# One pool of 2 KB slices for activations and split weights, and c loaded as one row, in a two-layer decoder trunk

## The chip, the cores and the metric

The kernel runs on one core of one Trainium2 chip. The metric is the time of one execution on the device in microseconds (us); lower is better. The engines are TensorE (PE in the profile; its weight loads are PEld), VectorE (DVE), ScalarE (ACT), GpSimd (POOL) and SyncE (SP), which issues nearly all transfers. SBUF, the working memory, is 128 partitions wide. PSUM, the matmul's output, has eight banks of 128 x 512 f32.

## The reference

Two layers act on x, 512 x 1024 f32. Each layer is a SwiGLU FFN with half weight, a token mixer, and a second such FFN. The mixer of layer 0 is a latent attention with 16 heads, and that of layer 1 is a dilated window attention with three groups of 16 heads. Each of the six sub-layers is wrapped in the same way:

```
mod = silu(c) @ w_mod[i] + b_mod[i]          # c: 1 x 1024, shift, scale, gate for each sub-layer
hn  = rmsnorm(x, pre_g) * (1 + scale) + shift
y   = rmsnorm(fn(hn), post_g)
x   = x + res_w * gate * y                   # res_w: 0.5 for FFNs, 1 for mixers

swiglu(h) = (silu(h @ w_gate) * (h @ w_up)) @ w_down      # D_FF = 2816
```

All inputs and parameters are f32.

## The kernel before

**Split products.** Every large product is three matmuls in a reduced f32 format (`mm3`, L141 to L146): both operands are split into a high part (a rounded copy) and a low part (the value minus the high part), and high x high, high x low and low x high are added in PSUM. The weights are split on the chip. `weights` (L123) loads a 128 x 1024 f32 block (512 KB) into a `raw` buffer (five of them), makes the high part with one ACT copy of 1024 columns (L128), and the low part with two DVE subtractions of 512 columns (L130). The parts go to the pool `ring`, six places of 4 KB per partition for `whi` and six for `wlo`. A second form, `Sliced` (L53 to L75), writes the parts as 512-column slices of 2 KB into the pool `sl` instead; it is used for the first weights of a sub-layer.

**The slices.** `sl` has 44 places of 2 KB (`t.s()`, L111). The modulated input h takes 16 (eight row blocks, high and low), the sub-layer's output y 8, a group of gated FFN rows up to 12, and the attention layers keep their queries, keys and values there.

**FFN.** The 22 column blocks of the hidden layer are taken in four groups (`GROUPS`). For each block, `head` forms gate and up products over eight k (48 matmuls of 512 columns) and the gated result. After a group, `down` adds its product with `w_down` for four row tiles. The last group's `down` is the tail of the sub-layer; `transition` (L458) weaves it with the norm of x, the turn of the next input (`turn`, L490: transposes on PE, then `modulate`), and the first heads of the next sub-layer.

**Order.** A planner (the Tile framework) orders each engine's instructions by the program's order and by its own estimate of when each can run, and places tiles in the pools. In `start` (L332) the order of SP, and for a stretch that of ACT and DVE, is as written out by hand.

**The start.** SP fetches c, broadcast to 128 partitions (512 KB written, L379), x tiles 0 and 1, the small vectors, the first block of `w_mod` for shift, x tile 2, the first block for scale, x tile 3, and both halves of the two weights of unit 0 (gate and up of block 0). ACT takes the silu of c (L396). `rise` (L352) handles one 128-row tile of x: ACT sums its squares, DVE adds them (L313), POOL raises to the power -1/2 (L314), DVE scales the tile (L364, L368), PE transposes it into eight PSUM banks (L370). `mod_fold` (L162) forms the dot of a `w_mod` block with the silu of c on DVE (L165) and adds the bias at once (`mod_out`, L168, L210). It stands behind tile 1 for shift and behind tile 2 for scale. Then the first 128 rows (k = 0) are modulated (L301 to L303), unit 0's halves are split (L68, L72), and `keep` (L374) copies the other banks to slices. Behind that a loop brings, for each further k, the four half blocks of `w_mod` (`mod_load`, L170), their dots (L180), the modulation, and the products of all units loaded so far; units 1 to 3 join after k = 1, 2 and 3.

```
rise(0); rise(1)
self.mod_fold(*mods[0], 0, raw[0])
rise(2)
self.mod_fold(*mods[1], 0, raw[1])
rise(3)
```

Of the kernel before, what the change touches and what calls it, by code (L numbers as in the profile page):

```python
# [24 lines left out]
RAW = 5  # L25
SLICES = 44
SLOTS = 6
KQ = 2
# [14 lines left out]

class Halves:
    def __init__(self, parts):
        self.parts = [x.rearrange("p (k c) -> p k c", c=P) for x in parts]

# [4 lines left out]

class Sliced:  # L53


    def __init__(self, t, src):
        self.t, self.src = t, src
        self.raw = t.ring.tile([P, CH], F32, tag="raw", name="raw", bufs=RAW)
        self.out = [[t.s(F32R), t.s(F32R)] for _ in range(2)]

    def at(self, j):
        return slice(j * SEQ, (j + 1) * SEQ)

    def fetch(self, j):
        self.t.nc.sync.dma_start(self.raw[:, self.at(j)], self.src[:, self.at(j)])

    def top(self, j):
        self.t.nc.scalar.activation(self.out[0][j], self.raw[:, self.at(j)], AF.Copy)  # L68

    def low(self, j):  # L70
        hi, lo = self.out
        self.t.nc.vector.tensor_tensor(lo[j], self.raw[:, self.at(j)], f(hi[j]), ALU.subtract)  # L72

# [4 lines left out]
class Trunk:  # L78
    def __init__(self, ctx, tc, a):
        self.ctx, self.tc, self.nc, self.a = ctx, tc, tc.nc, a  # L80
        nc = tc.nc
        self.cp = ctx.enter_context(tc.tile_pool(name="const", bufs=1))
        self.ring = ctx.enter_context(tc.tile_pool(name="ring", bufs=SLOTS))
        self.sl = ctx.enter_context(tc.tile_pool(name="sl", bufs=SLICES))
# [37 lines left out]

    def weights(self, src, flat=False):  # L123
        raw = self.load(src)
        n = src.shape[-1]
        hi = self.ring.tile([P, CH], F32R, tag="whi", name="whi")[:, :n]
        lo = self.ring.tile([P, CH], F32R, tag="wlo", name="wlo")[:, :n]
        self.nc.scalar.activation(hi, raw, AF.Copy)  # L128
        for r in (slice(0, n // 2), slice(n // 2, n)):
            self.nc.vector.tensor_tensor(lo[:, r], raw[:, r], f(hi[:, r]), ALU.subtract)  # L130
# [28 lines left out]
    def mod(self, l, n, k):  # L159
        self.mod_fold(l, n, k, self.load(self.a["w_mod"][l, n, k]))  # L160

    def mod_fold(self, l, n, k, raw):  # L162
        nc = self.nc
        t = self.tmp.tile([P, 2], F32, tag="mt", name="mt", bufs=4)
        nc.vector.tensor_tensor_reduce(  # L165
            raw, raw, self.cs, 1.0, 0.0, ALU.mult, ALU.add, accum_out=t[:, 0:1]
        )
        self.mod_out(l, n, k, t, lambda out, b: nc.vector.tensor_tensor(out, t[:, 0:1], b, ALU.add))  # L168

# [162 lines left out]
    def start(self, sub):  # L332
# [19 lines left out]
        def rise(i):  # L352
# [8 lines left out]
            else:  # L361
                self.square(x[1], t[1], ss[:, 1:2])
            r = self.scale_of(ss)
            nc.vector.tensor_scalar(t[0], x[0], r, None, ALU.mult)  # L364
            if last:
# [12 lines left out]
        self.first = sub  # L378
        nc.sync.dma_start(self.cs, self.a["c"].broadcast_to([P, D]))  # L379
# [12 lines left out]
        xt = [self.bank("mm" if k < 4 else "aux") for k in range(KT)]  # L392
        units, ks = [], []
        banks = {}
        with self.tc.manual_schedule(engines={ACT, DVE}):
            nc.scalar.activation(self.cs, self.cs, AF.Silu)  # L396
# [109 lines left out]
class Ffn:  # L506
# [10 lines left out]

    def gate_up_load(self, ft, sliced=False):
        t = self.t
        make = t.weights_sliced if sliced else t.weights  # L520
        self.w[ft] = [make(t.a["w_gu"][self.l, self.s, ft, g]) for g in range(2)]

    def prepare(self):
        self.gate_up_load(0, True)

# [49 lines left out]
    def down(self, q, i):  # L575
# [3 lines left out]
        if q not in self.wd:  # L579
            self.wd[q] = [  # L580
                t.weights(t.a["w_down"][self.l, self.s, at + j], flat=True) for j in range(m)
            ]
# [48 lines left out]
class Mixer:  # L631
# [5 lines left out]
    def out_weights(self, j):  # L637
        t = self.t
        if j not in self.wo:
            self.wo[j] = t.weights(t.a[self.w_o][j], flat=True)  # L640

    def products(self, b, i, d, js):
        t = self.t
        for j in js:
# [3 lines left out]
                [x[j][:, i * P : (i + 1) * P] for x in self.o],  # L648
                [x[:, d * SEQ : (d + 1) * SEQ] for x in self.wo[j]],
                j in (0, PART),  # L650
# [34 lines left out]
class Mla(Mixer):  # L685
# [37 lines left out]
    def prepare(self):  # L723
        self.w = {u: self.t.weights_sliced(self.t.a["mla_in"][u]) for u in range(2)}

# [30 lines left out]
    def value(self, j, e):  # L756
        t = self.t
        if not self.wv:
            self.wv += [t.weights(t.a["mla_v"][k], flat=True) for k in range(2)]
        b = t.bank()  # L760
        for k in range(2):
            ls = [x[:, j * P : (j + 1) * P] for x in self.latn[k]]
            t.mm3(b, ls, [x[:, e * SEQ : (e + 1) * SEQ] for x in self.wv[k]], k == 0, k == 1)
        self.v[j, e] = t.s()
# [163 lines left out]
class Dil(Mixer):  # L928
# [78 lines left out]
    def prepare(self):  # L1007
        t = self.t
        self.wt = {(0, u): t.weights_sliced(t.a["dil_in"][0, u]) for u in self.ORDER[:2]}

# [390 lines left out]
```

## Time and profile before

| | |
|---|---|
| time, median of 3 runs | 2277.34 us (2276.07 to 2277.81) |
| the profiled execution's own time | 2277.64 us |
| its span | 2275.9 us |
| PE busy | 2241.0 us, 98% |
| PE weight loads busy | 1853.5 us, 81% |
| DVE busy | 1203.6 us, 53% |
| ACT busy | 861.4 us, 38% |
| POOL busy | 106.1 us, 5% |
| mean granted clock of TensorE | 0.998 of full |

The span is the stretch that the profiler recorded; the time is a little longer. A row of the timeline has the start and the length in us, the engine, the source line, the operation, output and inputs, the shape and the count; in brackets stands how long the engine was idle before it and what ended that idle time. A row of the waits has engine, tile and line, what it waited for, and then the total in us, the number of times and the longest. A row of the groups has the busy time and the mean ns of one, and behind the bar the idle time before them and what ended it. A row of the stretches has the length, then the busy time (and count) of PE, PEld, DVE, ACT and POOL, the granted clock, the share of the transfer engines and GB/s. A row of the transfers has the count, the size, and the median us from issue to landing.

### The profile page before, as it was taken

The page shows a single profiled execution, that of the slowest core. Times are in us where ns is not written, and L with a number is a line of the kernel's source. Part 1 is how long each engine was busy: PE and PEld are TensorE (multiplying, and loading weights), DVE is VectorE, ACT ScalarE, POOL GpSimd, SP SyncE. Part 2 cuts the span into 40 slices and gives each one's busy share as a digit, 9 for nine tenths or more (in the row PEclk, how much of TensorE's full clock was granted, in tenths as well). Part 3 has the DMA queues.
Part 4 walks back from the last instruction along what each step waited for, and adds up shares of the span by engine and source line. Part 5 has one row for each costly group of instructions (what it writes and reads, how often), then busy time and mean ns, then how long its engine had stood idle before and what let it go on. Part 6 is the DMA issues. An engine that isn't in the chain of part 4 may idle for free. (4 is left out here: it accounts for less than half of the span.)

```text
span 2275.9 us, 30179 instructions
## 1 busy us (share of the span) xinstructions
PE 2241.0 (98%) x11418; PEld 1853.5 (81%) x11418; DVE 1203.6 (53%) x2711; ACT 861.4 (38%) x1751; POOL 106.1 (5%) x143
## 2 busy tenths in 40 slices
PE   6999999999999999999999999999999999999998
PEld 5888888877898888898888888777878878888887
DVE  7666566677665366474554473344334367243344
ACT  4432135577633132353222352444344345332232
POOL 0000001210110000020000010000000002000000
PEclk9999999999999999999999999999999999999999
DMA  8575662211255365344653523333333332242231
GB/s 311 162 251 183 186 231 69 99 47 56 70 172 184 93 208 176 107 140 123 192 175 114 155 93 105 80 95 88 83 89 80 96 79 79 75 130 98 79 111 37
DMA packets 121366, 284.56 MB, mean 125 GB/s; under 512 B 44145, under 2 KB 48516, under 8 KB 121220
## 3 DMA queue, kind: packets, MB, share of 16 engines
q1 hardware_dynamic: 121220, 282.63, 40.5%
q8 instruction: 89, 1.46, 0.3%
q14 instruction: 57, 0.47, 0.1%
HBM read 280.19 MB, written 2.39 MB: 124 GB/s over the span
## 5 line engine op out<-in xcount | busy, mean ns | idle before, releaser
L143 PE MATMUL mm<-s,whi 128*128 128x512 f32 (+1 forms) x2116 | 797.8, 378 | 3.7 <-ACT whi L128 2.5
L144 PE MATMUL mm<-s,whi 128*128 128x512 f32 (+1 forms) x2116 | 792.2, 374 | 0.0
L145 PE MATMUL mm<-s,wlo 128*128 128x512 f32 (+1 forms) x2116 | 791.5, 374 | 0.0
L128 ACT ACTIVATE whi<-raw 128x1024 fp32r<-128x1024 f32 (+1 forms) x356 | 369.7, 1053 | 973.2 <-PE mm L144 441.8
L130 DVE TENSOR_TENSOR wlo<-raw,whi 128x512 fp32r<-128x512 f32 (+1 forms) x712 | 466.0, 693 | 409.9 <-ACT whi L128 401.7
L143 PEld LDWEIGHTS mm<-s,whi 128*128 128x128 f32 x2116 | 399.3, 189 | 84.4 <-issue 7.0
L145 PEld LDWEIGHTS mm<-s,wlo 128*128 128x128 f32 x2116 | 399.6, 189 | 70.9
L144 PEld LDWEIGHTS mm<-s,whi 128*128 128x128 f32 x2116 | 399.5, 189 | 67.8
L143 PE MATMUL mm<-whi,s 128*128 128x512 f32 x848 | 332.4, 392 | 2.0 <-ACT s L679 1.3
L144 PE MATMUL mm<-wlo,s 128*128 128x512 f32 x848 | 330.4, 390 | 0.0
L145 PE MATMUL mm<-whi,s 128*128 128x512 f32 x848 | 330.1, 389 | 0.0
L165 DVE CUSTOM_DVE_ANT_0 raw<-raw,cs 128x1024 f32<-128x1024 f32 x130 | 160.1, 1236 | 108.5 <-DMA raw<-w_mod 107.9
L143 PEld LDWEIGHTS mm<-whi,s 128*128 128x128 f32 x848 | 159.2, 188 | 36.6 <-issue 2.5
L145 PEld LDWEIGHTS mm<-whi,s 128*128 128x128 f32 x848 | 159.2, 188 | 33.4 <-issue 0.3
L144 PEld LDWEIGHTS mm<-wlo,s 128*128 128x128 f32 x848 | 159.2, 188 | 32.6 <-issue 0.3
L554 DVE TENSOR_TENSOR gg<-silu,mm 128x512 f32<-128x512 f32 (+1 forms) x95 | 60.4, 635 | 172.2 <-PE mm L145 168.8
L444 DVE TENSOR_TENSOR s<-mm,s 128x512 f32<-128x512 f32 x112 | 76.5, 689 | 124.8 <-PE mm L145 124.7
L314 POOL TENSOR_TENSOR mv<-mv,mhalf 128x1 f32<-128x1 f32 x48 | 35.9, 750 | 1498.9 <-DVE mv L313 1496.4
L555 ACT ACTIVATE s<-gg 128x512 fp32r<-128x512 f32 (+1 forms) x97 | 57.4, 591 | 53.3 <-DVE gg L554 53.2
L552 ACT ACTIVATE silu<-mm 128x512 f32<-128x512 f32 (+1 forms) x95 | 51.4, 543 | 30.6 <-PE mm L145 30.5
L1040 ACT ACTIVATE s<-mm 128x512 f32<-128x512 f32 (+3 forms) x156 | 46.2, 374 | 34.8 <-PE mm L145 34.8
L448 ACT ACTIVATE s<-mm 128x512 f32<-128x512 f32 x40 | 23.8, 595 | 85.8 <-PE mm L145 85.5
(165 smaller groups left out, 1738.1 us busy)
## 6 DMA issues: line engine op xcount, KB each, us to landing
raw<-w_gu SPq DMA_DIRECT2D x168, 512.0 KB, 4.4
raw<-w_mod SPq DMA_DIRECT2D x130, 512.0 KB, 4.7
raw<-w_down SPq DMA_DIRECT2D x88, 512.0 KB, 4.3
raw<-dil_in SPq DMA_DIRECT2D x70, 512.0 KB, 3.6
s<-w_mod SPq DMA_DIRECT2D x28, 256.0 KB, 6.6
raw<-w_gu SPq DMA_DIRECT2D x16, 256.0 KB, 3.2
raw<-mla_o SPq DMA_DIRECT2D x8, 512.0 KB, 4.7
raw<-dil_o SPq DMA_DIRECT2D x8, 512.0 KB, 3.7
```

Source lines behind the costliest of these rows:

```text
L128: self.nc.scalar.activation(hi, raw, AF.Copy)
L130: self.nc.vector.tensor_tensor(lo[:, r], raw[:, r], f(hi[:, r]), ALU.subtract)
L143: mm(out, w[0], m[0], start=first, stop=False)
L144: mm(out, w[0], m[1], start=False, stop=False)
L145: mm(out, w[1], m[0], start=False, stop=last)
L165: nc.vector.tensor_tensor_reduce(raw, raw, self.cs, 1.0, 0.0, ALU.mult, ALU.add, accum_out=t[:, 0:1])
L314: nc.gpsimd.tensor_tensor(v[:, 1:2], v[:, 0:1], self.mhalf[:, 0:1], ALU.pow)
L444: nc.vector.tensor_tensor(y, b, y, ALU.add)
L552: nc.scalar.activation(s, banks[0], AF.Silu)
L554: nc.vector.tensor_tensor(v, s, banks[1], ALU.mult)
L555: nc.scalar.activation(ghi, v, AF.Copy)
L1040: nc.scalar.activation(out, src, AF.Copy)
```

## The change

The two forms of splitting become one. `Sliced` is renamed `Weights` and serves all weights: one fetch of the whole block, then for each half of 512 columns one ACT copy and one DVE subtraction into 2 KB slices. The pool `sl` has 68 places in place of 44; `whi` and `wlo` have no places any more. Products that read a weight by halves (`down`, the mixers' output products, `value`) take the slice of that half.

In the start, c is fetched as one row of 4 KB; two PE matmuls with a row of ones copy it to all partitions in two PSUM banks, and the silu reads it there in two halves. The fetches are in another order: row, x tile 0, shift block, x tile 1, scale block, x tiles 2 and 3, the small vectors, and the first halves of unit 0. The dot for shift stands behind tile 0 and that for scale behind tile 1. The bias sums of both stand in the last tile's `rise`, behind the request for its power. The second halves of unit 0 are fetched and split ahead of unit 2's weights.

```diff
-SLICES = 44
-SLOTS = 6
+SLICES = 68
-class Sliced:
+class Weights:
...
-    def fetch(self, j):
-        self.t.nc.sync.dma_start(self.raw[:, self.at(j)], self.src[:, self.at(j)])
+    def fetch(self, *js):
+        c = slice(self.at(js[0]).start, self.at(js[-1]).stop)
+        self.t.nc.sync.dma_start(self.raw[:, c], self.src[:, c])
...
-    def weights(self, src, flat=False):
-        raw = self.load(src)
-        n = src.shape[-1]
-        hi = self.ring.tile([P, CH], F32R, tag="whi", name="whi")[:, :n]
-        lo = self.ring.tile([P, CH], F32R, tag="wlo", name="wlo")[:, :n]
-        self.nc.scalar.activation(hi, raw, AF.Copy)
-        for r in (slice(0, n // 2), slice(n // 2, n)):
-            self.nc.vector.tensor_tensor(lo[:, r], raw[:, r], f(hi[:, r]), ALU.subtract)
-        return [t if flat else t.rearrange("p (k c) -> p k c", c=P) for t in (hi, lo)]
-
-    def weights_sliced(self, src):
-        w = Sliced(self, src)
+    def weights(self, src):
+        w = Weights(self, src)
+        w.fetch(0, 1)
         for j in range(2):
-            w.fetch(j)
             w.top(j)
             w.low(j)
         return w.parts()
...
+    def mod_dot(self, raw):
         nc = self.nc
         t = self.tmp.tile([P, 2], F32, tag="mt", name="mt", bufs=4)
         nc.vector.tensor_tensor_reduce(
             raw, raw, self.cs, 1.0, 0.0, ALU.mult, ALU.add, accum_out=t[:, 0:1]
         )
-        self.mod_out(l, n, k, t, lambda out, b: nc.vector.tensor_tensor(out, t[:, 0:1], b, ALU.add))
+        return t
+
+    def mod_sum(self, l, n, k, t):
+        add = self.nc.vector.tensor_tensor
+        self.mod_out(l, n, k, t, lambda out, b: add(out, t[:, 0:1], b, ALU.add))
...
             r = self.scale_of(ss)
+            if last:
+                for m, dot in zip(mods, dots):
+                    self.mod_sum(*m, 0, dot)
             nc.vector.tensor_scalar(t[0], x[0], r, None, ALU.mult)
...
-        nc.sync.dma_start(self.cs, self.a["c"].broadcast_to([P, D]))
+        row = self.tmp.tile([P, D], F32, tag="gb", name="gb", bufs=1)[0:1]
+        nc.sync.dma_start(row, self.a["c"])
         stream(0)
+        raw = [self.load(self.a["w_mod"][*mods[0], 0])]
         stream(1)
+        raw.append(self.load(self.a["w_mod"][*mods[1], 0]))
+        stream(2)
+        stream(3)
         nc.sync.dma_start(self.small, self.a["small"])
-        raw = [self.load(self.a["w_mod"][*mods[0], 0])]
-        stream(2)
-        raw.append(self.load(self.a["w_mod"][*mods[1], 0]))
-        stream(3)
-        w = [Sliced(self, self.a["w_gu"][sub.l, sub.s, 0, g]) for g in range(2)]
+        w = [Weights(self, self.a["w_gu"][sub.l, sub.s, 0, g]) for g in range(2)]
         sub.w[0] = [x.parts() for x in w]
-        for j in range(2):
-            for x in w:
-                x.fetch(j)
+        for x in w:
+            x.fetch(0)
+        cb = [self.bank("aux") for d in range(2)]
+        one = self.s()[0:1, :P]
+        nc.vector.memset(one, 1.0)
+        for d in range(2):
+            nc.tensor.matmul(cb[d], one, row[:, d * SEQ :][:, :SEQ], start=True, stop=True)
...
-            nc.scalar.activation(self.cs, self.cs, AF.Silu)
+            for d in range(2):
+                nc.scalar.activation(self.cs[:, d * SEQ :][:, :SEQ], cb[d], AF.Silu)
             self.new_h()
             rise(0)
+            dots = [self.mod_dot(raw[0])]
             rise(1)
-            self.mod_fold(*mods[0], 0, raw[0])
+            dots.append(self.mod_dot(raw[1]))
             rise(2)
-            self.mod_fold(*mods[1], 0, raw[1])
             rise(3)
...
             for k in range(2, 4):
                 keep(k)
-            for x in w:
-                x.top(1)
-                x.low(1)
             for k in range(4, KT):
                 keep(k)
...
             if kind:
+                if n == 2:
+                    for x in w:
+                        x.fetch(1)
+                        x.top(1)
+                        x.low(1)
                 sub.gate_up_load(n)
...
-                [x[:, d * SEQ : (d + 1) * SEQ] for x in self.wd[q][j]],
+                [x.slices[d] for x in self.wd[q][j]],
```

More of the change, by code (lines that the diff above doesn't have):

```diff
@@ L61, in at, with both @@
     def at(self, j):
-        return slice(j * SEQ, (j + 1) * SEQ)
-    def fetch(self, j):
-        self.t.nc.sync.dma_start(self.raw[:, self.at(j)], self.src[:, self.at(j)])
+        return slice(j * SEQ, min((j + 1) * SEQ, self.n))
+    def fetch(self, *js):
+        c = slice(self.at(js[0]).start, self.at(js[-1]).stop)
+        self.t.nc.sync.dma_start(self.raw[:, c], self.src[:, c])
+    def both(self, j):
+        n = self.at(j).stop - self.at(j).start
+        return [x[j][:, :n] for x in self.out]
     def top(self, j):
-        self.t.nc.scalar.activation(self.out[0][j], self.raw[:, self.at(j)], AF.Copy)
+        self.t.nc.scalar.activation(self.both(j)[0], self.raw[:, self.at(j)], AF.Copy)
     def low(self, j):
-        hi, lo = self.out
-        self.t.nc.vector.tensor_tensor(lo[j], self.raw[:, self.at(j)], f(hi[j]), ALU.subtract)
+        hi, lo = self.both(j)
+        self.t.nc.vector.tensor_tensor(lo, self.raw[:, self.at(j)], f(hi), ALU.subtract)
     def parts(self):
@@ L159, in mod @@
     def mod(self, l, n, k):
-        self.mod_fold(l, n, k, self.load(self.a["w_mod"][l, n, k]))
-    def mod_fold(self, l, n, k, raw):
+        self.mod_sum(l, n, k, self.mod_dot(self.load(self.a["w_mod"][l, n, k])))
+    def mod_dot(self, raw):
         nc = self.nc
@@ L580, in down @@
             self.wd[q] = [
-                t.weights(t.a["w_down"][self.l, self.s, at + j], flat=True) for j in range(m)
+                t.weights(t.a["w_down"][self.l, self.s, at + j]) for j in range(m)
             ]
@@ L648, in products @@
                 [x[j][:, i * P : (i + 1) * P] for x in self.o],
-                [x[:, d * SEQ : (d + 1) * SEQ] for x in self.wo[j]],
+                [x.slices[d] for x in self.wo[j]],
                 j in (0, PART),
@@ L723, in prepare @@
     def prepare(self):
-        self.w = {u: self.t.weights_sliced(self.t.a["mla_in"][u]) for u in range(2)}
+        self.w = {u: self.t.weights(self.t.a["mla_in"][u]) for u in range(2)}
     def norm(self, us, at, lo, hi):
@@ L758, in value @@
         if not self.wv:
-            self.wv += [t.weights(t.a["mla_v"][k], flat=True) for k in range(2)]
+            self.wv += [t.weights(t.a["mla_v"][k]) for k in range(2)]
         b = t.bank()
@@ L1008, in prepare @@
         t = self.t
-        self.wt = {(0, u): t.weights_sliced(t.a["dil_in"][0, u]) for u in self.ORDER[:2]}
+        self.wt = {(0, u): t.weights(t.a["dil_in"][0, u]) for u in self.ORDER[:2]}
     def tile(self, p, u, lo, hi):
```

16 lines of the change are left out of this document (8 added, 8 removed).

## The prediction

> **What bounds the kernel now.** I read the page's first part, then who TensorE (PE) waited for, then the busy time by stretches.
>
> ```profile
> span 2275.9 us, 30179 instructions
> PE 2241.0 (98%) x11418; PEld 1853.5 (81%) x11418; DVE 1203.6 (53%) x2711; ACT 861.4 (38%) x1751; POOL 106.1 (5%) x143
> ```
> ```profile
> PE mm L370 <- DVE s L364: 12.1, 3, 9.2
> ...
> PE mm L143 <- ACT whi L128: 2.5, 1, 2.5
> PE mm L143 <- ACT s L679: 1.3, 1, 1.3
> ```
> ```profile
> 200.00:2200.00 2000.00, 1989.69 (x10336) 1648.19 (x10335) 1041.54 (x2360) 775.58 (x1621) 95.35 (x126) 1.00 0.39 118
> 2255.00:2276.00 21.00, 13.65 (x61) 10.96 (x59) 9.81 (x16) 2.90 (x8) 1.75 (x3) 0.95 0.20 75
> ```
>
> PE is idle for 2275.9 - 2241.0 = 34.9 us of the span. 7.35 us of that is the end (21.00 - 13.65), 10.3 us lies scattered in the 2000 us of the middle, and the rest, some 17 us, in the start. In all the run PE waited once for a weight's copy (2.5 us, in the start), so deeper prefetch in the middle has nothing to win; PE's arithmetic is unchanged. What can be gained lies ahead of about 45 us, where PE has no data. The chain there is VectorE's (DVE):
>
> ```profile
> 5.14 1.06 ACT L396 ACTIVATE cs<-cs 128x1024 f32<-128x1024 f32 x1 [3.12 <-DMA cs<-c]
> 6.45 0.63 ACT L306 ACTIVATE s<-x 128x512 f32<-128x512 f32 x1 [0.26 <-DMA x<-x]
> 7.81 0.16 DVE L313 SCALAR_TENSOR_TENSOR mv<-ss 128x1 f32<-128x1 f32 x1 [6.91 <-ACT s L306]
> ...
> 10.64 0.63 ACT L306 ACTIVATE s<-x 128x512 f32<-128x512 f32 x1 [1.54 <-DMA x<-x]
> ...
> 11.06 1.22 DVE L165 CUSTOM_DVE_ANT_0 raw<-raw,cs 128x1024 f32<-128x1024 f32 x1
> ...
> 12.32 0.16 DVE L168 TENSOR_TENSOR mS<-mt,small 128x1 f32<-128x1 f32 x1
> 12.40 0.15 DVE L313 SCALAR_TENSOR_TENSOR mv<-ss 128x1 f32<-128x1 f32 x1
> ...
> 13.20 0.63 ACT L306 ACTIVATE s<-x 128x512 f32<-128x512 f32 x1 [1.22 <-DMA x<-x]
> ...
> 14.01 1.22 DVE L165 CUSTOM_DVE_ANT_0 raw<-raw,cs 128x1024 f32<-128x1024 f32 x1
> ...
> 15.55 0.69 DVE L358 CUSTOM_DVE_ANT_0 s<-x 128x512 f32<-128x512 f32 x1
> ...
> 17.17 0.49 DVE L364 TENSOR_SCALAR s<-x,mv 128x512 f32<-128x512 f32 x1 [0.66 <-POOL mv L314]
> ```
>
> From the first sum of squares (7.81) to the last tile's scaling (17.17) DVE is idle only in the four waits for POOL's power of some 0.66 us each. The last tile of x came at 13.20, yet DVE reached it at 15.55: its arrival does not bind, the first tile's does. And the first tile's squares (6.45) stood behind the silu of c, whose 512 KB came at 5.14.
>
> Behind it, DVE sets when each 128 rows k of the modulated input are there:
>
> ```profile
> 18.22 0.81 DVE L301 TENSOR_SCALAR u<-mm,mA,mS 128x512 f32<-128x512 f32 x1 [0.57 <-PE mm L370]
> ...
> 20.34 1.28 DVE L72 TENSOR_TENSOR s<-raw,s 128x512 fp32r<-128x512 f32 x2
> 22.23 1.29 DVE L72 TENSOR_TENSOR s<-raw,s 128x512 fp32r<-128x512 f32 x2 [0.60 <-ACT s L68]
> 23.44 0.69 DVE L180 CUSTOM_DVE_ANT_0 s<-s,cs 128x512 f32<-128x512 f32 x1
> ...
> 37.29 0.68 DVE L180 CUSTOM_DVE_ANT_0 s<-s,cs 128x512 f32<-128x512 f32 x1
> ...
> 43.12 2.74 DVE L130 TENSOR_TENSOR wlo<-raw,whi 128x512 fp32r<-128x512 f32 x4 [2.60 <-ACT whi L128]
> ...
> 50.17 0.69 DVE L303 TENSOR_TENSOR s<-u,s 128x512 fp32r<-128x512 f32 x1 [0.70 <-ACT s L302]
> ```
> ```profile
> 43.56 0.50 PE L144 MATMUL mm<-s 128*128 128x512 f32 x1 [0.41 <-POOL s L299]
> ...
> 51.64 0.39 PE L145 MATMUL aux<-s,wlo 128*128 128x512 f32 x1
> 51.87 0.39 PE L143 MATMUL mm<-s 128*128 128x512 f32 x1
> ```
>
> The dots of k = 1 begin at 23.44 and those of k = 3 at 37.29; the low part of k = 3 (POOL) ends PE's last wait of the start, at 43.56. After that PE has work without a break: the low part of k = 4 is done at 50.17 + 0.69 = 50.86, and PE asks for k = 4 only at 51.87. So what counts is how much earlier k = 3 comes.
>
> **The change part by part.** *c as one row.* 512 KB leave the queue ahead of x. At the start c came at 5.14, and the first x, 512 KB behind it, at 6.45: 1.31 us each. A zero-byte transfer in c's place would by that land at 3.83. Small transfers of the middle give the other end:
>
> ```profile
> x<-m SPq DMA_DIRECT2D x8, 8.0 KB, 1.7
> ```
> ```profile
> 0.74 0.39 SPq L379 DMA_DIRECT2D cs<-c  x1
> 1.18 0.90 SPq L350 DMA_DIRECT2D x<-x  x2
> ```
>
> Issued at 0.74 as c is now, that would be 2.44. I take 3.3, about midway. The first x keeps its issue at 1.18, 0.44 us behind where c's 512 KB were issued, so it lands some 0.44 behind c's 5.14, at 5.57; the later tiles, with w_mod between them, at 1.31 us each: the third, four transfers on, at 10.8 and the last at 12.1 (10.64 and 13.20 now); DVE gets to them later than that, as now.
>
> The row must now pass through two PE matmuls of 512 plain f32 columns into PSUM, ahead of the silu. No such matmul is in the start; the nearest rows are the scores of the attention, and the split matmuls of the first k, which run slower at the start:
>
> ```profile
> 550.55 1.98 PE L847 MATMUL mm<-s 96*128 96x512 f32 x4
> ```
> ```profile
> 21.67 0.63 PE L143 MATMUL mm<-s 128*128 128x512 f32 x1
> 22.10 0.63 PE L144 MATMUL mm<-s 128*128 128x512 f32 x1
> ```
> ```profile
> L847 PE MATMUL mm<-s 96*128 96x512 f32 x32 | 15.4, 602 | 0.0
> ```
>
> Four plain ones start (1.98 - 0.60) / 3 = 0.46 us apart, twice the 0.23 of the split ones in the same state (51.64 to 51.87). At the start the split ones are 0.43 apart, so plain ones 0.87, and 0.2 more till the result is out: both done 1.94 us after the row, 5.24. The second half's silu, in PSUM, costs as the copies there:
>
> ```profile
> 22.59 2.07 ACT L376 ACTIVATE s<-aux 128x512 f32<-128x512 f32 x4
> L68 ACT ACTIVATE s<-raw 128x512 fp32r<-128x512 f32 x24 | 13.4, 619 | 0.0
> ```
>
> 0.6 us: 5.85, and some 0.1 for two handovers. The squares begin at 5.95 against 6.45: **-0.5**. Bounds: row at 2.44, then x0 at 5.57 binds, -0.9; row at 5.14 as c now, both matmuls 7.1, silu 7.7, +1.25.
>
> [...]
>
> *Dots and sums.* Of the two folds, 11.06 to 12.40 and 14.01 to 15.55, the dots (1.22, next instruction 0.04 on) stay on DVE's chain between tiles, one place earlier each. The three small sums (0.16 each by L168) go behind the last tile's power, into its 0.66 us wait on POOL. Saved: 1.34 + 1.54 - 2 x 1.26 = **-0.36**. If POOL gave no cover it would be 0. w_mod for k = 0 comes one place ahead of each dot's need, and the sum's biases (small) at about 12.4.
>
> *The second weight halves of unit 0* leave the path to k = 1: DVE is free for its dots at 20.34 + 1.28 = 21.62 instead of 23.44: **-1.82**. Their two high copies on ScalarE (ACT) go too. Their data now comes after w_mod of k = 2; counting x 4, w_mod 2, small 0.2, unit 0's first halves 1, unit 1 and k = 1 and k = 2 with 2 each and the halves themselves 1, that is 14.2 transfers of 512 KB at 1.31 us behind 3.83 + 0.44, near 23 us. The step of DVE from the dots of k = 1 to those of k = 3 is 37.29 - 23.44 = 13.85 us, so k = 2's dots begin near 20.8 + 6.9 = 27.7, past that. They return as two subtractions ahead of k = 3: **+1.29**, ACT's 1.2 us in its idle time. SP passes the two fetches in order; unit 0's raw buffers, two of five, are held some 10 us longer, and the fetch of unit 2's second weight queues behind them on SP with w_mod of k = 3 behind it. That buffer comes free with unit 1's split, ahead of those 27.7 us; w_mod needs three transfers more, 3.9 us, to 31.6, and its dots begin at 35.9. No cost taken; the bound is the 2.60 us that DVE sat idle at 43.12.
>
> *Sum at k = 3:* -0.5 - 0.36 - 1.82 + 1.29 = **-1.4 us**, and k = 4 shifts with it. Ends: +1.25 - 0.36 - 1.82 + 1.29 = +0.4, and, if the planner puts the two subtractions behind the dots of k = 3, -0.9 - 0.36 - 1.82 = -3.1.
>
> *One pool.* The copies:
>
> ```profile
> L128 ACT ACTIVATE whi<-raw 128x1024 fp32r<-128x1024 f32 x348 | 362.6, 1057 | 967.9 <-PE mm L144 436.5 <-issue 258.2 <-PE mm L145 200.0
> ```
>
> 348 of them become two of 619 ns: 348 x (1.238 - 1.057) = 63 us more on ACT, which is idle for 1414 us and, ahead of these very copies, waits 637 us for PE to give a buffer back. Cost 0; if that cover went, no more than 0.18 us per weight. DVE's halves stay as they are. Places: 44 slices and 6 x 2 places of 4 KB were 136 KB, 68 slices are too. The fullest place is the hand-over between FFN layers: 12 of the last group, 8 of y, 16 of the new h and 8 of the next two weights were 44, beside six weights; now 44 + 24 = 68. While a group goes through the down product, 16 + 8 + 12 + 24 = 60 are held, so two more weights fit where there was place for none. PE waited for no weight there: 0, with the bound on the loss below.
>
> **The forecast:** the profiled execution took 2277.64 us, 1.74 above its span; 2277.64 - 1.4 = 2276.2. It lies 0.3 above the median of the runs, so 2275.9 there; I say 2276.
>
> **The rivals.** *Slower, late h at hand-overs.* h and the weights now draw on one pool. If the planner gives slices to the third weight before the 16 of h, h is written only when the down product frees slices, at its end, and PE waits.
>
> ```profile
> L301 DVE TENSOR_SCALAR u<-aux,mA,mS 128x256 f32<-128x256 f32 x60 | 30.8, 537 | 2.6 <-PE aux L497 1.8 <-POOL s L299 0.8
> L303 DVE TENSOR_TENSOR s<-u,s 128x256 fp32r<-128x256 f32 x60 | 25.2, 429 | 1.6 <-ACT s L302 1.0
> ```
>
> Six k's on DVE (the other two go over POOL) at 0.537 + 0.429 are 5.8 us per hand-over: 2276 + 5.8 = 2282 for one, 2305 for all five. It decides from the first slice of h granted late. For it: the copies' 637 us show weights always ready to take what is free. Against: h is asked for before those weights, and the count fits exactly.
>
> [...]
>
> *Faster, more than the start.* -3.1 there, and a third of the middle's 10.3 us gone because halves come free earlier: 2277.3 - 6.5 = 2270.8. Against: those waits are of 1.3 us or less (the longest by L679's row) and for results, not places.
>
> **How the numbers follow.** Forecast 0.45, no gain 0.13, slower 0.21, faster 0.21. A measurement can tell about 0.2% from no change, 4.6 us here: the forecast and the no-gain rival lie within it, less a little where the mid waits shift: same 0.55, faster 0.23, slower 0.22. The likeliest's own range is 2274 to 2278; for 8 in 10 it must reach most of the way to both other cases: 2269 to 2284.
>
> **What would show it.** First squares near 6.0 and the last tile's scaling near 16.3; the dots of k = 1 near 20.8; PE's wait for POOL on k = 3 ending near 42.2; no PE wait at a weight's copy; ACT busy near 925 us; PE idle in 200 to 2200 near 10 us. Wrong if the squares begin after 7, if PE waits for h at a hand-over, or if DVE waits for the late halves' data.

## The result and the profile after

The changed kernel takes **2849.38 us** (median of 4 runs, 2846.86 to 2854.95) against 2277.57 beside it: 1.2518 times as long, 95% interval 1.2503 to 1.2533. The prediction, 2276.0 with no real difference, was wrong by 573 us.

From the page of the changed kernel the busy times and three groups, then the span and the granted clock:

```profile
PE 2446.5 (86%) x11422; PEld 1915.1 (67%) x11422; DVE 1205.9 (42%) x2712; ACT 893.3 (31%) x2108; POOL 100.8 (4%) x143
...
L75 ACT ACTIVATE s<-raw 128x512 fp32r<-128x512 f32 x736 | 406.8, 618 | 21.9 <-DMA raw<-w_gu 14.9
L563 ACT ACTIVATE silu<-mm 128x512 f32<-128x512 f32 (+1 forms) x95 | 53.2, 560 | 629.0 <-PE mm L142 629.0
L566 ACT ACTIVATE s<-gg 128x512 fp32r<-128x512 f32 (+1 forms) x97 | 57.2, 590 | 496.7 <-DVE gg L565 484.5
...
core 0: 2853.2 us, clock 0.945
```

The span is 577.3 us longer. PE's idle time went from 34.9 to 2853.2 - 2446.5 = 406.7 us (+371.8), and PE is busy 205.5 us longer with the same products. A good half of that second part is clock: (1 - 0.945) x 2853 = 157 us of full-speed time were not granted, against 5 before (0.998), and by the granted clock in stretches of half a us some 121 of them fell while PE was busy, the rest while it was idle anyway. What makes up the other half was not traced.

PE's waits in the changed kernel (total, times, longest):

```profile
PE mm L140 <- ACT s L75: 253.2, 120, 12.2
PE mm L142 <- DVE s L79: 53.0, 27, 4.9
PE aux L1206 <- ACT sq L1151: 46.7, 8, 7.5
```

L75 is the ACT copy of half a weight, L79 the DVE subtraction behind it, and the third row is the exponentials of layer 1's attention. PE now waits for weights, which it did once in the kernel before, for 2.5 us. And ACT stands idle in other places than before: the copies of the kernel before (the row of L128 in the prediction) stood 967.9 us idle in front of a copy, mostly waiting for PE to give a place back. In the changed kernel the copies themselves wait for next to nothing (21.9 us); ACT stands in front of the silu (629.0) and in front of the high copy of the gated result (496.7). The weight copies come right behind that copy. One FFN block shows it, ACT first, then DVE, then PE's matmuls:

```profile
183.59 0.60 ACT L563 ACTIVATE silu<-mm 128x512 f32<-128x512 f32 x1 [5.10 <-PE mm L142]
189.76 0.63 ACT L566 ACTIVATE s<-gg 128x512 fp32r<-128x512 f32 x1 [5.57 <-DVE gg L565]
190.30 2.17 ACT L75 ACTIVATE s<-raw 128x512 fp32r<-128x512 f32 x4
...
206.79 0.63 ACT L566 ACTIVATE s<-gg 128x512 fp32r<-128x512 f32 x1 [5.57 <-DVE gg L565]
207.33 1.14 ACT L75 ACTIVATE s<-raw 128x512 fp32r<-128x512 f32 x2
```
```profile
189.04 0.69 DVE L565 TENSOR_TENSOR gg<-silu,mm 128x512 f32<-128x512 f32 x1 [1.27 <-PE mm L142]
191.05 1.23 DVE L162 CUSTOM_DVE_ANT_0 raw<-raw,cs 128x1024 f32<-128x1024 f32 x1 [1.32 <-DMA raw<-w_mod]
...
192.88 0.68 DVE L79 TENSOR_TENSOR s<-raw,s 128x512 fp32r<-128x512 f32 x1
```
```profile
190.97 0.50 PE L140 MATMUL mm<-s 128*128 128x512 f32 x1 [2.03 <-ACT s L75]
...
193.62 0.68 PE L142 MATMUL mm<-s 128*128 128x512 f32 x1 [1.92 <-DVE s L79]
194.10 0.63 PE L140 MATMUL mm<-s 128*128 128x512 f32 x1
194.52 0.63 PE L141 MATMUL mm<-s 128*128 128x512 f32 x1
...
197.60 0.40 PE L140 MATMUL mm<-s 128*128 128x512 f32 x1
197.83 0.40 PE L141 MATMUL mm<-s 128*128 128x512 f32 x1
...
207.99 0.50 PE L140 MATMUL mm<-s 128*128 128x512 f32 x1 [2.03 <-ACT s L75]
```

Read it as a chain. PE ends the block; DVE forms the gated product (189.04); ACT copies its high part (189.76); only then, with no gap, ACT copies the next block's weights (190.30), and PE, 2.03 us idle, begins (190.97). On DVE, a modulation dot that waited for its transfer (191.05) stands in front of the first low part (192.88), so PE waits another 1.92 us. Then the matmuls come 0.42 us apart (194.10, 194.52) and 3.5 us later 0.23 (197.60, 197.83): half the rate for some 3 us, at a granted clock of 0.50 from 194 to 197. From block to block it is 207.99 - 190.97 = 17.02 us. In the kernel before, ACT's timeline in a block of the same FFN shows one weight copied in the middle of the block, ahead of the gated result, as soon as PE gave a place back, and 150.78 - 139.90 = 10.88 us from silu to silu:

```profile
139.90 0.58 ACT L552 ACTIVATE silu<-mm 128x512 f32<-128x512 f32 x1
144.32 1.06 ACT L128 ACTIVATE whi<-raw 128x1024 fp32r<-128x1024 f32 x1 [3.84 <-PE mm L144]
146.74 0.63 ACT L555 ACTIVATE s<-gg 128x512 fp32r<-128x512 f32 x1 [1.35 <-DVE gg L554]
...
150.78 0.58 ACT L552 ACTIVATE silu<-mm 128x512 f32<-128x512 f32 x1
```

The clock shows by itself in the stretches of another place, where PE had waited 4.59 us up to 126.74 (columns as in the prediction; the granted clock is the third number from the right):

```profile
125.00:129.00 4.00, 2.26 (x5) 1.82 (x6) 3.45 (x7) 0.00 (x0) 0.00 (x0) 0.56 0.00 0
129.00:133.00 4.00, 4.00 (x12) 3.14 (x11) 0.00 (x0) 0.00 (x0) 0.00 (x0) 0.58 0.60 132
133.00:137.00 4.00, 4.00 (x20) 3.27 (x19) 0.00 (x0) 0.60 (x1) 0.00 (x0) 1.00 0.96 383
```

12 matmuls instead of 20 in 4 us that all count as busy, with granted clocks of 0.56 and 0.58 in the first two stretches and 1.00 in the third. In this trace the granted clock goes down, among other moments, at 125.5, 142.57 and 193.77 and up again at 132.33, 149.40 and 197.18, so it was lower for 6.83, 6.83 and 3.41 us. PE had not stood idle all the time ahead of that: in the 3.41 us up to 142.57 it worked for 0.9 us, and in those up to 193.77, around the second wait above, for 0.9 us too. From 77 us on, the clock goes down 57 times in the run, and in the 3.41 us ahead of each PE was busy for at most 1.71 us. As little work did not always cost clock: in the 3.42 us up to 207.99 PE was busy for 1.39 us, and the granted clock stayed at 1.00. So one wait of some 2 us went with a slow stretch and another did not: the wait up to 207.99 cost none.

The time can be laid out by stages, with the attention's scores of layer 0 (L847 before, L858 after) and of layer 1 (Dil; L1075, L1086) as marks. A column is what lies between two marks, so the ends of a mixer stand in the columns beside it. First and last of their matmuls, before and then after:

```profile
L847 PE MATMUL mm<-s x128: 272/432/697, 448.5 to 568.3; 96*128 96x128 f32 x32, 96*128 96x256 f32 x32, 96*128 96x384 f32 x32, 96*128 96x512 f32 x32
L1075 PE MATMUL mm<-s x384: 272/272/480, 1403.0 to 1845.7; 64*128 64x128 f32 x144, 64*128 64x256 f32 x48
```
```profile
L858 PE MATMUL mm<-s x128: 272/468/697, 564.3 to 687.5; 96*128 96x128 f32 x32, 96*128 96x256 f32 x32, 96*128 96x384 f32 x32, 96*128 96x512 f32 x32
L1086 PE MATMUL mm<-s x384: 272/272/480, 1714.3 to 2345.0; 64*128 64x128 f32 x144, 64*128 64x256 f32 x48
```

| us of the span | first FFN | attention | two FFNs | Dil | last FFN | all |
|---|---|---|---|---|---|---|
| before | 448.5 | 119.8 | 834.7 | 442.7 | 430.2 | 2275.9 |
| after | 564.3 | 123.2 | 1026.8 | 630.7 | 508.2 | 2853.2 |
| start_only | 447.6 | 119.8 | 834.7 | 441.2 | 429.2 | 2272.5 |
| own_places | 450.6 | 120.0 | 835.7 | 441.0 | 427.5 | 2274.8 |
| g_apart | 469.4 | 124.7 | 848.7 | 630.4 | 447.2 | 2520.4 |
| ask_ahead | 497.7 | 124.6 | 885.3 | 627.4 | 464.2 | 2599.2 |
| ask_both | 494.7 | 124.7 | 892.6 | 521.5 | 460.1 | 2493.6 |
| dil_two | 495.8 | 123.2 | 891.0 | 487.1 | 463.6 | 2460.7 |
| no_dots | 526.6 | 123.2 | 969.9 | 630.3 | 507.9 | 2757.9 |
| two_no_dots | 484.0 | 124.7 | 885.8 | 487.6 | 463.5 | 2445.6 |

The loss lies in all FFNs (115.8 + 192.1 + 78.0) and in Dil (188.0), and hardly in the attention (3.4). The lower rows are the experiments'.

### The profile page after: what moved, and what is told of

Read it like the earlier page. It is cut to its first block, busy times and chain, and to the rows that moved or that the text cites. A ratio compares the mean times of both kernels' runs of the same rounds, so it can differ in the third digit from the quotient of the medians.

```text
span 2853.2 us, 30307 instructions
## 1 busy us (share of the span) xinstructions
PE 2446.5 (86%) x11422; PEld 1915.1 (67%) x11422; DVE 1205.9 (42%) x2712; ACT 893.3 (31%) x2108; POOL 100.8 (4%) x143
## 4 chain that ended last, share of the span: by engine, by line
PE 62%; DMA 13%; DVE 12%; ACT 7%; issue 4%; POOL 1%; SPq 1%; DVEq 0%; POOLq 0%; ACTq 0%
PE mm L142 20%; PE mm L140 19%; PE mm L141 18%; DMA raw<-w_mod 8%; DVE s L79 3%; DVE raw L162 2%; DVE gg L565 2%; ACT s L75 2%; ACT s L566 1%; PE mm L858 1%; ACT sq L1151 1%; ACT u L1151 1%; ACT s L1051 1%; PE mm L1086 1%; POOL mv L315 1%
## 5 line engine op out<-in xcount | busy, mean ns | idle before, releaser
L140 PE MATMUL mm<-s 128*128 128x512 f32 (+1 forms) x3140 | 1224.0, 394 | 260.8 <-ACT s L75 253.2
L142 PE MATMUL mm<-s 128*128 128x512 f32 (+1 forms) x3140 | 1219.8, 390 | 56.1 <-DVE s L79 53.0
L141 PE MATMUL mm<-s 128*128 128x512 f32 (+1 forms) x3140 | 1209.3, 387 | 4.4 <-DVE s L304 2.0
L140 PEld LDWEIGHTS mm<-s 128*128 128x128 f32 x3140 | 616.3, 196 | 422.4 <-ACT s L75 308.3
L142 PEld LDWEIGHTS mm<-s 128*128 128x128 f32 x3140 | 616.0, 196 | 211.8 <-DVE s L79 105.3
L141 PEld LDWEIGHTS mm<-s 128*128 128x128 f32 x3140 | 615.4, 196 | 121.9 <-DVE s L79 4.9
L79 DVE TENSOR_TENSOR s<-raw,s 128x512 fp32r<-128x512 f32 x736 | 467.6, 686 | 334.7 <-ACT s L75 334.3
L75 ACT ACTIVATE s<-raw 128x512 fp32r<-128x512 f32 x736 | 406.8, 618 | 21.9 <-DMA raw<-w_gu 14.9
L565 DVE TENSOR_TENSOR gg<-silu,mm 128x512 f32<-128x512 f32 (+1 forms) x95 | 60.5, 637 | 536.9 <-PE mm L142 520.3
L563 ACT ACTIVATE silu<-mm 128x512 f32<-128x512 f32 (+1 forms) x95 | 53.2, 560 | 629.0 <-PE mm L142 629.0
L566 ACT ACTIVATE s<-gg 128x512 fp32r<-128x512 f32 (+1 forms) x97 | 57.2, 590 | 496.7 <-DVE gg L565 484.5
L568 DVE TENSOR_TENSOR s<-gg,s 128x512 fp32r<-128x512 f32 x79 | 54.7, 692 | 44.2 <-ACT s L566 44.1
L1206 PE MATMUL aux<-ident,sq 128*128 128x128 f32 x112 | 30.7, 418 | 46.9 <-ACT sq L1151 46.7
L1206 PEld LDWEIGHTS aux<-ident,sq 128*128 128x128 f32 x112 | 16.2, 190 | 64.4 <-ACT sq L1151 58.5
L1151 ACT ACTIVATE u<-u,y 128x128 f32<-128x128 f32 x128 | 49.4, 387 | 21.0 <-DVE y L1132 21.0
L1210 DVE COPY silu<-aux 128x512 f32<-128x512 f32 x32 | 21.3, 687 | 77.7 <-PE aux L1206 76.1
L1086 PE MATMUL mm<-s 64*128 64x128 f32 (+1 forms) x384 | 46.4, 324 | 0.0
```

What stands on the lines that cost most here:

```text
L75: self.t.nc.scalar.activation(self.both(j)[0], self.raw[:, self.at(j)], AF.Copy)
L79: self.t.nc.vector.tensor_tensor(lo, self.raw[:, self.at(j)], f(hi), ALU.subtract)
L140: mm(out, w[0], m[0], start=first, stop=False)
L141: mm(out, w[0], m[1], start=False, stop=False)
L142: mm(out, w[1], m[0], start=False, stop=last)
L565: nc.vector.tensor_tensor(v, s, banks[1], ALU.mult)
```

## The experiments

The theory: slices of one pool are given out in the order in which the program asks for them, and one that is asked for holds back those behind it until it is first written. In `gate_up_out` a block asks for the slices of its gated result, written when the block is done; the next block asks for its weights behind that. With places of their own the weights pass it; in one pool they can't. Rivals: the places are too few, or the copies as halves cost, or the start does.

**Which part: the start or the pool.** `start_only` is the kernel before with the changed start (row of c, order of fetches, dots and sums, late halves) and its old pools; `pool_only` is the changed kernel with the old start. Each carries one half of the diff shown ahead of the prediction.

> The kernel before with only the change's start: c as one row through two matmuls, the new order of fetches, the dots ahead of the last tile, the late second halves of unit 0; weights keep their own places. If the shared pool is what costs, this is within 2 us of before or up to 2 us faster (the changed kernel's trace has the first modulated rows of k = 1 on PE at 25.78 instead of 27.97 and those of k = 2 at 33.30 instead of 34.89). If the start is what costs, it is near 2850 us.

> The changed kernel with the start of before (c broadcast by the transfer, folds behind tiles 1 and 2, unit 0's halves split together); one pool of 68 slices. If the shared pool costs: 2845 to 2856 us. If the start costs: near 2277 us.

Measured: start_only 2274.15 us (2272.29 to 2275.74), 0.9991 [0.9982, 1.0000] of before; pool_only 2841.94 in one run, 3 us under its range. The loss comes with the pool, and without it the new start costs nothing.

**Number or order of places.** `own_places` keeps the copies as halves and all 68 places of 2 KB, but 24 of them are for weights alone (the weights fetched by `prepare`, ahead of a sub-layer, stay in the 44, as before):

```diff
-SLICES = 68
+SLICES = 44
+WSLICES = 24
...
+    def w(self, dtype=F32):
+        return self.sl.tile([P, SEQ], dtype, tag="w", name="w", bufs=WSLICES)
...
-        self.out = [[t.s(F32R), t.s(F32R)] for _ in range(2)]
+        new = t.w if own else t.s
+        self.out = [[new(F32R), new(F32R)] for _ in range(2)]
```

`g_apart` does the reverse for one kind only: the gated rows get 12 places of their own, and everything else, weights included, shares 56.

```diff
-                x.append(t.s(F32R))
+                x.append(t.g(F32R))
```

> The changed kernel with the same 68 slices, but 24 of them under a tag of their own for the weights that had the ring, 44 for the rest. Theory A (slices of one tag are given in the order in which the program asks, so a block's weights queue behind the gated result of the block before): back to 2273 to 2279 us. Theory B (68 slices are too few for how long things are held): no gain, at or above 2800 us, since the sum of places is the same and each part has fewer to draw on. Theory C (two copies of 512 columns in place of one of 1024, and the later release, hold ACT and DVE up): stays far above 2277, over 2500 us.

> The changed kernel with only the gated FFN rows under a tag of their own (12 slices), 56 for all else, the weights among them. Theory A: the FFN stages lose nearly all their waits for weight copies (116, 192 and 78 us over before in the three stretches around the two attentions), the dilated attention keeps its 188 us: 2440 to 2520 us. Theory B: as slow as the change or slower, 2840 us or more.

Measured: own_places **2275.79** (2273.87 to 2277.39), 0.9995 [0.9986, 1.0004]; g_apart 2522.45 in one run. With the same number of places, the same halves and the same start the loss is gone as soon as weights need not stand in one order with the rest. PE's one wait for a weight in own_places, and the group of the copies:

```profile
PE mm L145 <- ACT w L77: 1.0, 1, 1.0
```
```profile
L77 ACT ACTIVATE w<-raw 128x512 fp32r<-128x512 f32 x712 | 440.2, 627 | 951.4 <-PE mm L146 828.3 <-issue 74.7 <-DMA raw<-w_gu 38.0
```

The copies wait for PE to give a place back again, as before, and not behind results. g_apart, 2 us above its range, gives the FFNs most of their loss back (two FFNs: 848.7, with 834.7 before and 1026.8 after) and Dil nothing (630.4), as it must if each stage has late slices of its own.

**Only the order of asking.** `ask_ahead` is the changed kernel, one pool of 68, with the next block's weights asked for before this block's gated result:

```diff
         self.gate_up_mm(ft, lo, hi, banks, range(KT))
+        if hi == SEQ and ft + 1 < FT and ft + 1 not in self.w:
+            self.gate_up_load(ft + 1)
         self.gate_up_out(ft, lo, hi, banks)
```

`ask_both` does the same in Dil: a tile asks for the next tile's weight ahead of its own result. `dil_two` asks there for the next two tiles' weights.

```diff
+            if hi == SEQ:
+                for step in (1, 2):
+                    n_p, at = divmod(9 * p + self.ORDER.index(u) + step, 9)
+                    n_u = self.ORDER[at]
+                    if n_p < 8 and (n_p, n_u) not in self.wt:
+                        self.wt[n_p, n_u] = t.weights(t.a["dil_in"][n_p, n_u])
             self.qkv[p, u] = t.s()
```

> The changed kernel, one pool of 68 slices, no place added; in the FFN the next block's two weights are asked for ahead of this block's gated result. Theory A (slices are given in the order of asking): the FFN stretches lose most of their 386 us, the dilated attention keeps its 188: 2480 to 2580 us, near the 2522 of the run with the gated rows apart. Theory B (too few places): asking earlier holds more, 2850 us or more.

> As the run before it, and in the dilated attention too the next tile's weight is asked for ahead of this tile's result. Theory A: the dilated stretch, 631 us in the change and 443 in the kernel before, falls below 560 (other late-written slices, the bias rows and the reciprocals that come through memory, are still asked for in between), the whole to 2330 to 2470 us. Theory B: no gain over the run before it.

> The changed kernel with one pool of 68; a feed-forward block asks for the next block's weights ahead of its own gated result (as in ask_ahead), and in Dil a tile asks for the weights of the next two tiles ahead of its own result (ask_both: one). If what is left of Dil's loss (521.5 us with one tile ahead, 442.7 before) is still a weight's slices standing behind bias rows, values and reciprocals that are written late, a second tile of lead covers it: Dil 445 to 480 us, the whole 2420 to 2455. If what is left is something else than the order of asking (places, the copies as halves), two tiles ahead hold 4 more slices and Dil stays at 515 to 560, the whole 2490 to 2540.

Measured, one run each: 2600.96, 2495.5 and 2462.43. Neither the places nor the work changed, only where the program asks: the two FFNs come back from 1026.8 to 885.3, Dil from 630.7 to 521.5 and to 487.1. PE's waits for L75 fall from 253.2 to 95.2, 72.3 and 69.6 us, and those for Dil's exponentials, 45.8 us in ask_ahead, fall to 12.6 and 0.3 once Dil asks earlier too: they hung on the same order. The edit moves the whole call, so the fetch, the copies and the subtractions stand earlier in the program too; that it is the pool and not this order alone follows from own_places, where no call moved. That a slice holds back others until its first write, and not by some other rule of the planner, was not tried by itself. All three stopped short of what was expected: ask_ahead and ask_both by 21 and 26 us, dil_two by 7, all of it in Dil (445 to 480 expected). What is left in dil_two's two FFNs shows in PE's timeline. Between 680 and 1500 nine waits of over 1.5 us remain, eight of them of this form; two that follow each other, and then SP and ACT at the first of them:

```profile
832.05 1.02 PE L140 MATMUL mm<-s 128*128 128x512 f32 x2 [2.03 <-ACT s L75]
923.95 1.32 PE L140 MATMUL mm<-s 128*128 128x512 f32 x2 [2.03 <-ACT s L75]
```
```profile
815.38 18.37 SPq L68 DMA_DIRECT2D raw<-w_down  x6
```
```profile
830.85 0.63 ACT L566 ACTIVATE s<-gg 128x512 fp32r<-128x512 f32 x1 [5.57 <-DVE gg L565]
831.38 5.30 ACT L75 ACTIVATE s<-raw 128x512 fp32r<-128x512 f32 x10
```

They are no longer 17 us apart but 92, and eight is the number of groups in two FFNs: it is where the down product's weights, fetched from 815 on, are still asked for behind the group's last gated result, and copied ten halves in a heap behind it. These eight waits are 16 of the 56 us that the two FFNs still lack (891.0 against 834.7). PE's idle time there is 36 us in all; of the rest, which is PE's busy time, part is the clock (0.99), and the whole was not traced. In Dil of dil_two, PE's waits between 1510 and 1997 and DVE in front of one of them:

```profile
PE mm L142 <- DVE s L79: 29.0, 7, 4.8
```
```profile
1761.40 0.17 DVE L1186 TENSOR_TENSOR w<-x 128x8 f32<-128x8 f32 x1 [1.69 <-DMA x<-z]
...
1761.82 0.20 DVE L1188 RECIPROCAL w<-w 128x8 f32<-128x8 f32 x1
1761.94 3.65 DVE L79 TENSOR_TENSOR s<-raw,s 128x512 fp32r<-128x512 f32 x6
```

Seven times, once per pair of heads but the last, six subtractions come in one heap behind reciprocals whose sums return from memory. That is 29 of the 44 us that Dil still lacks; the rest goes with granted clocks of 0.93 to 0.98 there. That it is again a slice asked for early and written late (the softmax's reciprocals and the bias rows take slices too) fits, but was not tried apart; that the planner merely put the subtractions behind the reciprocals on DVE fits as well.

**The modulation dots.** In the block above, a dot that waits for its transfer stood ahead of a weight's low part. `no_dots` leaves out 128 of the 130 full-width modulation dots, with their transfers; the sums take a zero, and the output is another. `two_no_dots` does the same to dil_two.

```diff
-        self.mod_sum(l, n, k, self.mod_dot(self.load(self.a["w_mod"][l, n, k])))
+        t = self.tmp.tile([P, 2], F32, tag="mt", name="mt", bufs=4)
+        self.nc.vector.memset(t[:, 0:1], 0.0)
+        self.mod_sum(l, n, k, t)
```

> The changed kernel without 128 of its 130 modulation dots and their transfers of 512 KB (the modulation is then from the biases alone, so its output differs). Theory A: each block still pays the two microseconds from the end of its up product to the next block's first copy, and the clock's slow spells behind it; what goes is the time in which a subtraction or a gated product stood behind a dot on DVE: 2500 to 2700 us. Theory D (the dots, late because weights hold the raw buffers longer, are the cause): below 2350 us.

> dil_two without the 128 modulation dots of the middle and their transfers (the sums take a zero instead; the output is another). If the feed-forward blocks' remaining loss (885 us between MLA and Dil with the next block's weights asked ahead, 835 before) is VectorE standing in front of modulation weights that come late, it goes: 835 to 850 us there, and the whole 90 or more below dil_two. If the dots only stood where VectorE would have waited in any case, the feed-forward stretch stays at 875 to 890 and the whole falls by less than 25.

Measured, one run each: 2759.74 and 2447.39. Without dots the changed kernel is 90 us faster, less than the theory allowed them, and far from repaired: its waits for L75 are still there,

```profile
PE mm L140 <- ACT s L75: 211.5, 120, 8.9
```

120 times as with the dots. So the dots add to the loss and do not cause it. Once weights are asked for a block ahead, they are worth only 15 us, 12 of them in the first FFN and 5 in the two FFNs between, against the 90 expected if they were the rest of the FFNs' loss. That guess fell; the group boundaries above explain part of that rest.

**The start, tuned further.** start_only showed the first squares at 6.65, no earlier than before. `silu_late` is start_only with the silu of c behind the first tile's squares on ACT (shown against start_only):

```diff
-            for d in range(2):
-                nc.scalar.activation(self.cs[:, d * SEQ :][:, :SEQ], cb[d], AF.Silu)
             self.new_h()
             rise(0)
+            for d in range(2):
+                nc.scalar.activation(self.cs[:, d * SEQ :][:, :SEQ], cb[d], AF.Silu)
```

`dots_inside` also moves the two dots into the waits of tiles 1 and 2 for POOL's power, and `own_inside` is own_places with that start.

```diff
             r = self.scale_of(ss)
+            if i in (1, 2):
+                dots.append(self.mod_dot(raw[i - 1]))
```

> The kernel before with the change's start alone, and the silu of c behind the first tile's squares on ACT instead of ahead of them. The squares then start when x lands, near 5.6 instead of 6.75, and DVE's chain moves with them by 1.1 us: 2272 to 2274 us, 1 us less than the start alone. Rival: DVE's chain is then bound by the dot, which needs the silu: no change from 2274.2.

> silu_late (the kernel before with the changed start, the silu of c behind the first tile's squares) with the two modulation dots of k = 0 put between a tile's sum of squares and its scaling, where VectorE waits for GpSimd's power. If VectorE's chain to k = 3 sets PE's start, the two waits of 0.66 us are gone: the last tile's scaling near 14.5 (15.7 in silu_late), 2271.7, that is 0.9976 of before. If the tiles of x or the squares bind by then: the scaling near 15.5, 2273, no change against silu_late.

> own_places (the changed kernel with 24 of its 68 places for weights alone) with the start of dots_inside. If the pool as such costs and brings nothing once weights have their own places, this is dots_inside to within 1.5 us: 2271 to 2273.5. If one pool of 2 KB places is a small loss (own_places stood 1.6 us above start_only): 2273.5 to 2275.

Measured: silu_late **2273.04** (2271.24 to 2275.02), 0.9986 [0.9976, 0.9995]; dots_inside 2273.96 (2271.84 to 2275.03), 0.9989 [0.9980, 0.9997]; own_inside 2275.10 (2273.86 to 2277.87), 0.9995 [0.9986, 1.0004], 0.1 above the upper of its two ranges. silu_late lies below both kernels of this case, below the kernel before by some 3 us (0.14%, with an interval that ends just short of no change). ACT's timeline in it:

```profile
4.76 0.63 ACT L310 ACTIVATE s<-x 128x512 f32<-128x512 f32 x1 [2.74 <-DMA x<-x]
...
6.11 1.28 ACT L411 ACT_TABLE_LOAD   x1
7.40 1.08 ACT L411 ACTIVATE cs<-aux 128x512 f32<-128x512 f32 x2
8.37 0.63 ACT L310 ACTIVATE s<-x 128x512 f32<-128x512 f32 x1
```

The squares are 1.9 us earlier, but a second table load stands in front of the silu, and tile 1's squares begin at 8.37 where start_only had them at 8.11. In dots_inside, DVE therefore waits for tile 1's squares and gains nothing from the room it made:

```profile
9.83 0.16 DVE L317 SCALAR_TENSOR_TENSOR mv<-ss 128x1 f32<-128x1 f32 x1 [1.90 <-ACT s L310]
...
16.51 0.49 DVE L373 TENSOR_SCALAR s<-x,mv 128x512 f32<-128x512 f32 x1 [0.33 <-POOL mv L318]
```

The last tile's scaling is at 16.51, later than silu_late's 15.74: the second expectation of the two, and more. The three intervals overlap, so between these starts, and on whether one pool size costs 1 us (own_places against start_only, own_inside against dots_inside), the runs decide nothing.

## Why the prediction was wrong, and where it was right

**The step that failed is "One pool ... Cost 0".** Alone, in pool_only, it cost 566 us (2841.94 against 2276.06), of a miss of 573. It was argued from the number of places (44 + 24 = 68 at the fullest point) and from ACT's cover (1414 us idle, 637 us waiting for PE). Both statements are true, and own_places shows that neither costs: the same 68 places, the same 2 KB copies, ACT busy 928.9 us (925 was foretold), and 2275.79 us. What the step left out is who stands ahead of whom. Two pools had let a weight pass a result that is not there yet; one pool makes the weight wait for it. "PE waited for no weight there" measured the old order and could not tell of the new one. The cover was real only as long as the copies could be issued at any time in a block: in the changed kernel ACT has more idle time than before (1960 us against 1414), but 1126 of it lie ahead of the silu and the gated copy and 467 ahead of Dil's results. The sign that told was "no PE wait at a weight's copy": there are 120.

Much of the price could have been estimated from the kernel before. Once weights stand behind the gated result, a block adds to PE's time the chain of product, high copy and first weight copy (0.69, 0.63 and 0.62 us by the rows of L565, L566 and L75, whose forms the kernel before has too). That is some 2 us, for 22 blocks in each of four FFNs 176 us, without the clock and Dil. Of PE's 253.2 us for L75 some 228 lie in the three FFN columns and some 26 in Dil.

**The slower rival** was of the right kind, one pool and the order in which it is granted, and had the wrong side. It let h stand behind weights, at five hand-overs, for 5.8 us each; the trace has weights behind results, in block after block. Its own argument against itself ("h is asked for before those weights") named the mechanism, a result asked for ahead of weights, but saw it only for h, not for the gated result. Both the forecast's range and this rival's 2305 us at most fell far short.

**"c as one row: -0.5" failed in a term.** The row was sooner than taken, and the matmuls twice as long:

```profile
2.47 3.75 PE L400 MATMUL aux<-gb,s 1*128 1x512 f32 x4 [2.47 <-DMA gb<-c]
```
```profile
4.55 0.60 ACT L406 ACTIVATE cs<-aux 128x512 f32<-128x512 f32 x1 [2.54 <-PE aux L400]
6.26 0.60 ACT L406 ACTIVATE cs<-aux 128x512 f32<-128x512 f32 x1 [1.11 <-PE aux L400]
6.75 0.62 ACT L307 ACTIVATE s<-x 128x512 f32<-128x512 f32 x1
```

The row lands at 2.47 (3.3 was taken, 2.44 was the lower end). The two matmuls are four instructions and 3.75 us, not 1.94: the scores' "x4" that I read as four matmuls were two, each in two instructions (L847 has x32 of 512 columns for 16 heads). The squares begin at 6.75, 0.3 later than before and not 0.5 earlier. The first x was sooner than taken too, there by 4.76 in silu_late and not at 5.57; here the silu hid it.

**What held.** In the changed kernel DVE's chain keeps its other steps to within some tenths:

```profile
16.88 0.48 DVE L368 TENSOR_SCALAR s<-x,mv 128x512 f32<-128x512 f32 x1 [0.33 <-POOL mv L315]
...
21.25 0.68 DVE L181 CUSTOM_DVE_ANT_0 s<-s,cs 128x512 f32<-128x512 f32 x1
...
37.50 0.69 DVE L181 CUSTOM_DVE_ANT_0 s<-s,cs 128x512 f32<-128x512 f32 x1
```
```profile
43.78 0.50 PE L141 MATMUL mm<-s 128*128 128x512 f32 x1 [0.41 <-POOL s L300]
```

The last scaling came 0.29 earlier with squares 0.30 later: -0.59 for dots and sums (-0.36 foretold). The dots of k = 1 came 2.19 earlier (16.3 and 20.8 were named for the two, 16.88 and 21.25 measured; the squares, late by the row's matmuls, stood 0.8 behind their forecast). From there to the dots of k = 3 it is 16.25 us against 13.85, 2.4 more, not the 1.29 that the return of the late halves was to cost; all of the gain is gone by k = 3 (37.50 against 37.29, and PE's wait for POOL ends at 43.78 against 43.56, where 42.2 was foretold). With the old pools the same stretch takes 15.84 (start_only's dots at 21.16 and 37.00), so 0.7 of the miss is the start's own; what it consists of was not traced. start_only's -1.9 us stands near the -1.4 foretold for the start, yet its dots of k = 3 are only 0.29 earlier, not 1.4, and its interval reaches to no change: the nearness is luck.

## What to carry to other kernels

Before merging two pools, list for each stage what asks for places in which order and when each is first written; a place asked for early and written late holds back everything asked for behind it, however many places are free. Equal bytes do not mean equal freedom: give operands that can be fetched ahead places apart from results, or ask for them first. And if an engine's idle time is to cover added work, check that the work can still be issued in that idle time after the change.

## What the runs showed of the hardware

A loss of this kind is paid in part twice: beside 372 us more of idle time, the repeated waits went with some 121 us of clock lost while PE was busy. Each of the 57 times that the clock went down after 77 us, PE had been busy for at most 1.71 of the 3.41 us ahead. An f32 matmul of 512 columns was two instructions here and took 1.7 to 1.9 us at the start (two took 3.75 us, and the silu of the first half could begin 2.08 us after the row had landed). And the silu moved behind squares on ACT cost a table load of 1.28 us (6.11 in silu_late), although the kernel's first load (0.74 in start_only) had served both when the silu came first.
